# Delta layer of a two-layer decoder trunk: the lower off-diagonal block of the 64-row inverses by a DVE transposition in place of eight matrix products and a copy

## The chip, the cores and the metric

One core of a Trainium2 chip runs the whole program. The metric is device time in microseconds of one execution; three runs of the kernel before gave the median that a changed kernel is held against.

## The reference, cut to what matters

Two layers, a sparse attention and a gated delta rule, each followed by a gated embedding. The change is in the delta rule, where for each head and each chunk of rows a unit lower triangular system is solved:

```python
lower = jnp.where(strict, jnp.einsum("bhntd,bhnjd->bhntj", kb, kc) * decay, 0.0)
a_mat = lower + jnp.eye(CHUNK)
rhs = jnp.concatenate([vc * bc[..., None], kb * jnp.exp(gc)[..., None]], axis=-1)
sol = lax.linalg.triangular_solve(a_mat, rhs, left_side=True, lower=True)
...
def step(state, xs):                      # over the chunks of a head, in order
    u = u_p - w_d @ state
    o = q_d @ state + a_qk @ u
    state = state * cd + k_d.T @ u
```

## The kernel before, in words

The kernel takes chunks of 128 rows, so a half of the sequence has eight chunks per head (NC = 8), and 8 heads times 2 halves make 16 rounds, j = 0 to 15, in the function `phase4`. In a round four things are woven together on the engines' queues: `project(j)` (the products pBk, pBq, pBz, pBv of 128x512, lines L1521 to L1523, three for each of 8 blocks of the input), `within(j-1)` and `beside(j-1)` (the inverses and the other preparations of a head), `across(j-2)` (the recurrence over the chunks: pks, y, pu, uu, po, state, lines L1747 to L1766), and `gated(j-3)` (the output's norm and transposition, pot). Which instruction comes when on an engine follows from the yielded positions and from the scheduler that the program is built with; each engine then takes its own list in order. After the last rounds `ahead` puts the first products of the next stage (poe, L90 to L92) between what is left of the recurrence, and `wout` prepares their weights: an ACT copy (L78, L86) and a subtraction on DVE (L79) or POOL (L87) for each piece of `wo`.

`within` inverts the eight 128x128 triangles of a head at once. The 32x32 diagonal blocks are inverted on DVE (L1632 to L1642), go through DRAM and come back as Uc, the upper triangular form (U), whose transposed blocks are Tc (L1652). Then blocks of 32 are merged to 64, and 64 to 128. With X = (L block) times (T block) on PE (px, L1664, copied by ACT on L1665), the off-diagonal block of U is X-transposed times Uc (pd, L1673, eight products of 32x32 for each p, copied to U by ACT on L1674). For p = 0 the same block is also wanted transposed, in the tile T64, since the merge of 64 to 128 multiplies with it (px_1, L1684, copied by ACT on L1685; pd_2, L1689, copied by ACT on L1690). Before the change that transposed block is computed by itself: eight products more with the operands exchanged (L1677), into the other partitions of the same PSUM tile pd, and a DVE copy (L1678).

Of the kernel before, what the change touches and what calls it, by code (L numbers as in the profile page):

```python
# [27 lines left out]
NC = 8  # L28
# [10 lines left out]
def tile_trunk(ctx: ExitStack, tc: tile.TileContext, a: dict, out: bass.AP):  # L39
    nc = tc.nc  # L40
# [17 lines left out]
    def T(tag, bufs, shape, name, dt=F32, where=None):  # L58
        return (where or pools[-1]).tile(shape, dt, tag=tag, bufs=bufs, name=name)
# [7 lines left out]
    def ps(tag, bufs, name, cols=512):  # L67
        return psum.tile([P, cols], F32, tag=tag, bufs=bufs, name=name)
# [1308 lines left out]
    def phase4():  # L1377
# [10 lines left out]
        T64 = T("T64", 1, [64, NC, 64], "T64")  # L1388
# [164 lines left out]
        def within(j):  # L1553
# [80 lines left out]
            for t in range(0, 32, 2):  # L1634

                n, m_ = t + 2, (t + 1) // 4 + 1
# [9 lines left out]
            Uc, Tc = T("Uc", 1, [P, NC, 32], f"Uc{j}"), T("Tc", 1, [P, NC, 32], f"Tc{j}")  # L1646
# [10 lines left out]
            X = T("tmp", 1, [P, NC, 32], f"X{j}_0")  # L1657
            q = [slice(b * 32, (b + 1) * 32) for b in range(4)]
            for p in range(2):
                e, o = q[2 * p], q[2 * p + 1]  # L1660
# [7 lines left out]
            for p in range(2):  # L1668
                e, o = q[2 * p], q[2 * p + 1]
                yield LV + 0.06 + p * 0.02  # L1670
                pd = ps("g", 3, f"pd{j}_{p}")
                for c in range(NC):
                    nc.tensor.matmul(pd[e, c * 32:(c + 1) * 32], X[o, c], Uc[o, c], start=True, stop=True)  # L1673
                nc.scalar.activation(U[e, :, o], pd[e, :NC * 32].rearrange("p (c n) -> p c n", c=NC), AF.Copy)  # L1674
                if p == 0:
                    for c in range(NC):
                        nc.tensor.matmul(pd[o, 256 + c * 32:256 + (c + 1) * 32], Uc[o, c], X[o, c], start=True, stop=True)  # L1677
                    nc.vector.tensor_copy(T64[o, :, 0:32], pd[o, 256:].rearrange("p (c n) -> p c n", c=NC))  # L1678

            lo, hi = slice(0, 64), slice(64, P)  # L1680
            yield LV + 0.14
            px, X = ps("g", 3, f"px{j}_1"), T("blk", 1, [P, NC, 64], f"X{j}_1")
# [144 lines left out]
        n = 2 * H  # L1827
        for j in range(n + 2):
            o_ = [gated(j - 3, 0.1)] if 3 <= j <= n else []
            if j == n + 1:  # L1830
                o_ = [gated(n - 2, 0.0, True)]
            a_ = [across(j - 2)] if j >= 2 else []
            if j == n + 1:
                a_ = [itertools.chain(a_[0], gated(n - 1, 0.97, True))]
            weave(*a_, *o_, *([within(j - 1), beside(j - 1)] if 1 <= j <= n else []),
                  project(j) if j < n else ahead(j - n))
# [87 lines left out]
```

## Time and profile before

| | |
|---|---|
| three runs, median (lowest to highest) | 3437.28 us (3433.69 to 3441.73) |
| the profiled execution: time, and span in the trace | 3443.02 us, 3441.3 us |
| PE busy, DVE busy, ACT busy, POOL busy | 96%, 61%, 54%, 28% of the span |
| mean granted TensorE clock | 0.982 |
| rounds of the delta stage (from the first L1664 to the last L1689) | 1937 to 3036 us, about 69 us each |

The profiled execution is one run more, with the profiler on. Busy shares are means over a span whose stages differ; the rows that bear on the change are in the section before the prediction.

### The profile page before, as it was taken

To read this page: it belongs to the slowest core of one execution; us is meant where nothing else is said; L and a number is where in the kernel's file an instruction comes from. 1 tells how busy PE (TensorE), PEld (TensorE's weight loads), DVE (VectorE), ACT (ScalarE), POOL (GpSimd) and SP (SyncE) were. 2 spreads that over 40 slices of the span, in tenths; PEclk is the share of its full clock that TensorE was granted. 3 is DMA by queue.
4 is the path that set the end of the run, shared out by engine and by line. 5 is a ranking of instruction groups with operands and counts; after the bars stand their busy time and mean duration, and the time that the engine had idled before them with its cause. 6 is when DMAs were issued, how large, how long until landed. Compare 5 with 4: busy or idle time off the path is not lost.

```text
span 3441.3 us, 51940 instructions
## 1 busy us (share of the span) xinstructions
PE 3304.1 (96%) x18954; PEld 2773.9 (81%) x18954; DVE 2090.1 (61%) x4502; ACT 1862.2 (54%) x3255; POOL 950.1 (28%) x1620
## 2 busy tenths in 40 slices
PE   8999989998899999999999999999999999899999
PEld 6778877887799999888887788887788888678887
DVE  5347996773688888522134577677577677733222
ACT  5356958664677777533335465555565556434221
POOL 2022535246454445211100221231121232321100
PEclk9999999999999999999999999999999999999999
DMA  7532465443422222422222222222222222243212
GB/s 244 178 112 70 128 209 164 168 155 120 152 79 84 79 76 78 159 73 72 66 81 79 51 50 56 53 59 81 62 50 56 53 59 50 86 133 115 74 35 71
DMA packets 327596, 328.46 MB, mean 95 GB/s; under 512 B 69704, under 2 KB 273064, under 8 KB 323240
## 3 DMA queue, kind: packets, MB, share of 16 engines
q1 hardware_dynamic: 327336, 325.11, 31.1%
q8 instruction: 149, 2.44, 0.3%
q14 instruction: 111, 0.91, 0.1%
HBM read 221.24 MB, written 103.81 MB: 94 GB/s over the span
## 4 chain that ended last, share of the span: by engine, by line
PE 54%; DVE 11%; DMA 4%; POOL 2%; ACT 2%; issue 2%; SPq 0%; DVEq 0%; ACTq 0%; POOLq 0%
PE pgm L91 3%; PE pgm L92 3%; PE pgm L90 3%; PE pt L1024 3%; DVE tmp L1639 2%; PE pom L90 2%; PE pom L92 2%; PE pom L91 2%; PE pBv L1521 2%; PE po L1044 2%; PE pBv L1522 2%; PE po L1045 2%; PE lg L92 2%; PE pBv L1523 2%; PE lg L90 2%
## 5 line engine op out<-in xcount | busy, mean ns | idle before, releaser
L79 DVE TENSOR_TENSOR pl<-pt,ph 128x512 fp32r<-128x512 f32 (+1 forms) x288 | 187.7, 658 | 47.3 <-ACT ph L78 45.1
L78 ACT ACTIVATE ph<-pt 128x512 fp32r<-128x512 f32 (+1 forms) x288 | 159.8, 564 | 97.7 <-PE pt L1024 89.0
L1006 ACT ACTIVATE pr<-pr,nm,qscale 128x1024 f32<-128x1024 f32 (+2 forms) x192 | 189.5, 988 | 40.7 <-DVE nm L1003 39.7
L1247 DVE TENSOR_TENSOR gm<-ppm,gm 128x512 f32<-128x512 f32 x64 | 43.4, 690 | 244.3 <-ACT gm L1246 244.3
L423 DVE SCALAR_TENSOR_TENSOR score<-rl,wi,score 128x1024 f32<-128x1024 f32 (+7 forms) x154 | 170.0, 1127 | 35.2 <-ACT rl L415 34.3
L415 ACT ACTIVATE rl<-il 128x1024 f32<-128x1024 f32 (+7 forms) x176 | 142.7, 817 | 74.8 <-PE il L92 69.0
L1024 PE MATMUL pt<-ident,pr 128*128 128x128 f32 x1088 | 169.7, 276 | 8.2 <-ACT pr L1006 5.5
L90 PE MATMUL pom<-wo,ym 128*128 128x512 f32 x432 | 171.1, 396 | 1.9 <-DVE y L1056 1.1
L91 PE MATMUL pom<-wo,ym 128*128 128x512 f32 x432 | 169.4, 392 | 1.3 <-POOL wo L87 1.3
L91 PE MATMUL pgm<-wm,xh 128*128 128x512 f32 x432 | 168.9, 391 | 1.6 <-DVE wm L82 1.6
L729 DVE TENSOR_SCALAR_CACHE_REDUCE tkj<-score,t 128x1664 bf16<-128x1664 f32 (+3 forms) x91 | 121.9, 1353 | 79.0 <-POOL t L769 69.9
L90 PE MATMUL pgm<-wm,xh 128*128 128x512 f32 x432 | 169.0, 391 | 0.7 <-ACT gm L1246 0.6
L92 PE MATMUL pom<-wo,ym 128*128 128x512 f32 x432 | 169.2, 392 | 0.0
L92 PE MATMUL pgm<-wm,xl 128*128 128x512 f32 x432 | 169.0, 391 | 0.0
L1044 PE MATMUL po<-pl,kv 128*128 128x256 f32 x576 | 163.2, 283 | 1.7 <-DVE pl L79 1.6
L1045 PE MATMUL po<-ph,kv 128*128 128x256 f32 x576 | 162.3, 282 | 0.0
L1043 PE MATMUL po<-ph,kv 128*128 128x256 f32 x576 | 161.4, 280 | 0.8 <-ACT ph L78 0.6
L87 POOL TENSOR_TENSOR ym<-yr,ym 128x1024 fp32r<-128x1024 f32 x32 | 77.1, 2409 | 304.7 <-ACT ym L86 304.5
L1246 ACT ACTIVATE gm<-pgm,rm_r 128x512 f32<-128x512 f32 x64 | 42.9, 684 | 183.7 <-PE pgm L91 117.4
L727 ACT ACTIVATE tkj<-score,t 128x1920 bf16<-128x1920 f32 (+3 forms) x91 | 127.8, 1405 | 26.7 <-POOL t L769 13.6
L1752 ACT ACTIVATE qs<-pks,eg 128x128 f32<-128x128 f32 x120 | 44.0, 366 | 179.6 <-DVE y L1749 173.6
L90 PE MATMUL lg<-kv,q 128*128 128x512 f32 (+2 forms) x320 | 139.7, 437 | 0.7 <-DVE mx L997 0.7
(636 smaller groups left out, 10814.6 us busy)
## 6 DMA issues: line engine op xcount, KB each, us to landing
wBr<-in_b_w_in_dram SPq DMA_DIRECT2D x64, 512.0 KB
wr<-in_a_w_in_dram SPq DMA_DIRECT2D x74, 256.0 KB
hT_d<-hT SPq DMA_DIRECT2D x32, 512.0 KB
hz<-hT_d SPq DMA_DIRECT2D x16, 1024.0 KB
yr<-yT_d SPq DMA_DIRECT2D x32, 512.0 KB
x<-in_x_dram SPq DMA_DIRECT2D x16, 512.0 KB
zT_d<-z SPq DMA_DIRECT2D x32, 256.0 KB
k_d<-k SPq DMA_DIRECT2D x16, 512.0 KB
```

What stands on the lines that cost most here:

```text
L78: nc.scalar.activation(hi, src, AF.Copy)
L79: nc.vector.tensor_tensor(lo, src, f32(hi), ALU.subtract)
L90: nc.tensor.matmul(dst, ah, bh, start=first, stop=False)
L91: nc.tensor.matmul(dst, ah, bl, start=False, stop=False)
L92: nc.tensor.matmul(dst, al, bh, start=False, stop=last)
L415: nc.scalar.activation(rl[:, :s1 - s0], pl[:, :s1 - s0], AF.Relu)
L423: nc.vector.scalar_tensor_tensor(sc[:, s0:s1], rl[:, :s1 - s0], w, sc[:, s0:s1], ALU.mult, ALU.add)
L1006: nc.scalar.activation(pr[:, s0:s1], pr[:, s0:s1], AF.Exp, bias=nm, scale=sc, accum_out=den[:, i % 2, x:x + 1])
L1024: nc.tensor.transpose(pt[:, x * P:(x + 1) * P], probs[h, i][:, j * P:(j + 1) * P], ident)
L1043: nc.tensor.matmul(d, V[0][:, j], ph[:, c], start=st, stop=False)
L1044: nc.tensor.matmul(d, V[0][:, j], pl[:, c], start=False, stop=False)
L1045: nc.tensor.matmul(d, V[1][:, j], ph[:, c], start=False, stop=sp)
```

## The change

The eight products L1677 and the copy L1678 go. In their place one DVE transposition of 32x32 blocks reads pd[e], the product that stands in PSUM already for U, and writes T64. Behind it all source lines move up by two, so L1684 of before is L1682 of the changed kernel, L1790 is L1788, and so on.

```diff
                 nc.scalar.activation(U[e, :, o], pd[e, :NC * 32].rearrange("p (c n) -> p c n", c=NC), AF.Copy)
                 if p == 0:
-                    for c in range(NC):
-                        nc.tensor.matmul(pd[o, 256 + c * 32:256 + (c + 1) * 32], Uc[o, c], X[o, c], start=True, stop=True)
-                    nc.vector.tensor_copy(T64[o, :, 0:32], pd[o, 256:].rearrange("p (c n) -> p c n", c=NC))
+                    nc.vector.transpose(T64[o, :, 0:32], pd[e, :NC * 32].rearrange("p (c n) -> p c n", c=NC))
```

On PE, in the round whose products stand at 2019 to 2029 us in the trace (j = 1), the queue holds before (pBv are the products of `project`; of the trace's names the numbers are left out):

```order
L1673 MATMUL pd_0_22236<-Uc_22158,X_0_22189 32x32 x8
L1673 MATMUL pd_1_22261<-Uc_22158,X_0_22189 32x32 x8
L1521 MATMUL pBv_1_22287<-hB_0_20410,wB_22127 128x512
L1522 MATMUL pBv_1_22287<-hB_0_20410,wB_22127 128x512
L1677 MATMUL pd_0_22236<-X_0_22189,Uc_22158 32x32 x8
L1523 MATMUL pBv_1_22287<-hB_0_20410,wB_22127 128x512
L1521 MATMUL pBv_1_22287<-hB_0_20410,wB_22127 128x512
L1522 MATMUL pBv_1_22287<-hB_0_20410,wB_22127 128x512
L1523 MATMUL pBv_1_22287<-hB_0_20410,wB_22127 128x512
L1521 MATMUL pBv_1_22287<-hB_1_20411,wB_22127 128x512
L1684 MATMUL px_1_22298<-T_20782,LT_21695 64x64 x8
```

and with the change:

```order
L1673 MATMUL pd_0_22228<-Uc_22150,X_0_22181 32x32 x8
L1673 MATMUL pd_1_22245<-Uc_22150,X_0_22181 32x32 x8
L1521 MATMUL pBv_1_22271<-hB_0_20410,wB_22119 128x512
L1522 MATMUL pBv_1_22271<-hB_0_20410,wB_22119 128x512
L1523 MATMUL pBv_1_22271<-hB_0_20410,wB_22119 128x512
L1521 MATMUL pBv_1_22271<-hB_0_20410,wB_22119 128x512
L1682 MATMUL px_1_22282<-T_20782,LT_21687 64x64 x8
```

L1677 is gone, and px_1 stands behind four large products after the pd blocks where it stood behind seven; it is the same in most rounds.

On DVE, in the same round, with the engines that each row waits for, before:

```order
L1667 COPY T_20782<-Tc_22159 32x8x32
L1466 SCALAR_TENSOR_TENSOR vT_22176<-xbv_0_22282,b_conv_w,vT_22176 128x512 [waits Activation_49,Pool_49]
L1466 SCALAR_TENSOR_TENSOR vT_22176<-xbv_0_22282,b_conv_w,vT_22176 128x512 [waits DVE_49] x2
L1678 COPY T_20782<-pd_0_22236 32x8x32 [waits PE_49,Activation_49]
L1774 TENSOR_REDUCE ss_22348<-o_22426 128x8 [waits Activation_49]
```

and with the change:

```order
L1667 COPY T_20782<-Tc_22151 32x8x32
L1466 SCALAR_TENSOR_TENSOR vT_22168<-xbv_0_22266,b_conv_w,vT_22168 128x512 [waits Activation_49,Pool_49]
L1466 SCALAR_TENSOR_TENSOR vT_22168<-xbv_0_22266,b_conv_w,vT_22168 128x512 [waits DVE_49]
L1676 STREAM_TRANSPOSE T_20782<-pd_0_22228 32x8x32 [waits Activation_49]
L1466 SCALAR_TENSOR_TENSOR vT_22168<-xbv_0_22266,b_conv_w,vT_22168 128x512 [waits DVE_49]
L1772 TENSOR_REDUCE ss_22332<-o_22410 128x8 [waits Activation_49]
```

The transposition stands one tap of the convolution (L1466) earlier than the copy did, and it waits for ACT, which reads the same block of pd for U.

In the last round (within of j = 15, about 2957 to 2985 us) the lists of POOL, DVE, ACT and PE are put in another order too. On POOL, before (kt and vt are scalings of a head's keys and outputs, wo the weights of the next stage, blk and ym copies for what follows):

```order
L1715 TENSOR_SCALAR kt_31416<-kt_31416,dT_31449 128x128 x8
L87 TENSOR_TENSOR wo_0_31450<-wor_3_31556,wo_0_31450 128x1024
L87 TENSOR_TENSOR wo_4_31577<-wor_5_31628,wo_4_31577 128x1024
L1790 TENSOR_SCALAR vt_30312<-vt_30312,rs_31419 128x128 x8
L87 TENSOR_TENSOR wo_4_31577<-wor_7_31684,wo_4_31577 128x1024
L1712 AFFINE_SELECT aq_31527<-aq_31527 128x1024
```

and with the change:

```order
L1713 TENSOR_SCALAR kt_31296<-kt_31296,dT_31329 128x128 x8
L1788 TENSOR_SCALAR vt_30208<-vt_30208,rs_31299 128x128 x8
L87 TENSOR_TENSOR wo_0_31330<-wor_3_31436,wo_0_31330 128x1024
L87 TENSOR_TENSOR wo_4_31457<-wor_5_31508,wo_4_31457 128x1024
L1710 AFFINE_SELECT aq_31407<-aq_31407 128x1024
L1622 COPY blk_31374<-blk_31374 32x1024 x2
```

The scaling of vt now stands ahead of the pair of wo subtractions instead of behind it. In the same place PE now takes pot and pqs ahead of pu of chunk 1 (it stood behind), and DVE takes a subtraction of its own, wo_4 (L79), ahead of the state of chunk 1 instead of ahead of pot's evictions.

## Rows read from the trace of the kernel before

**Rows 1.** The page: span, and busy time of each engine.

```profile
span 3441.3 us, 51940 instructions
PE 3304.1 (96%) x18954; PEld 2773.9 (81%) x18954; DVE 2090.1 (61%) x4502; ACT 1862.2 (54%) x3255; POOL 950.1 (28%) x1620
```

**Rows 2.** Windows: length, then busy of PE, PEld, DVE, ACT, POOL; clock, DMA.

```profile
1937.00:1956.00 19.00, 18.41 (x113) 13.12 (x114) 4.45 (x7) 3.73 (x7) 2.05 (x7) 0.55 0.15 29
2030.00:2099.00 69.00, 67.73 (x455) 56.29 (x454) 48.51 (x111) 39.09 (x74) 16.89 (x38) 1.00 0.22 55
2970.00:2987.00 17.00, 14.12 (x59) 12.37 (x60) 9.51 (x22) 5.60 (x10) 7.55 (x11) 0.50 0.56 168
3036.00:3441.00 405.00, 397.10 (x1832) 326.37 (x1830) 108.64 (x183) 117.94 (x183) 47.26 (x44) 1.00 0.26 82
```

**Rows 3.** Waits of PE, 1937 to 2957 us: total, times, longest.

```profile
PE pu L1755 <- DVE y L1749: 11.6, 15, 1.0
PE pot L1547 <- POOL vt L1790: 4.8, 12, 0.4
```

**Rows 4.** Timeline of PE in round 1: start, duration, engine, line, operation.

```profile
2021.15 1.09 PE L1673 MATMUL pd<-Uc,X 32*32 32x32 f32 x32
...
2022.51 0.40 PE L1522 MATMUL pBv<-hB,wB 128*128 128x512 f32 x1
2022.84 0.69 PE L1677 MATMUL pd<-X,Uc 32*32 32x32 f32 x16
2023.45 0.50 PE L1523 MATMUL pBv<-hB,wB 128*128 128x512 f32 x1
2023.79 0.39 PE L1521 MATMUL pBv<-hB,wB 128*128 128x512 f32 x1
2024.02 0.40 PE L1522 MATMUL pBv<-hB,wB 128*128 128x512 f32 x1
...
2024.81 1.14 PE L1684 MATMUL px<-T,LT 64*64 64x64 f32 x16
```

**Rows 5.** Timeline of all engines there: DVE and ACT rows.

```profile
2020.23 2.38 DVE L1466 SCALAR_TENSOR_TENSOR vT<-xbv,b_conv_w,vT 128x512 f32<-128x512 f32 x3
...
2021.87 0.78 ACT L1674 ACTIVATE U<-pd 32x256 f32<-32x256 f32 x2 [0.90 <-PE pd L1673]
...
2023.63 0.42 DVE L1678 COPY T<-pd 32x256 f32<-32x256 f32 x1 [1.02 <-PE pd L1677]
```

**Rows 6.** Line L1652, the transposition there is: duration ns min/median/max.

```profile
L1652 DVE STREAM_TRANSPOSE Tc<-Uc x16: 431/432/445, 1937.0 to 3025.6; 128x256 f32<-128x256 f32 x16
```

**Rows 7.** Timeline of PE in round 0, around L1677.

```profile
1946.16 0.63 PE L1523 MATMUL pBv<-hB,wB 128*128 128x512 f32 x1
...
1947.71 0.80 PE L1521 MATMUL pBv<-hB,wB 128*128 128x512 f32 x1
...
1948.31 0.63 PE L1522 MATMUL pBv<-hB,wB 128*128 128x512 f32 x1
1948.73 0.63 PE L1523 MATMUL pBv<-hB,wB 128*128 128x512 f32 x1
```

**Rows 8.** Timeline of PE in round 7, behind L1677.

```profile
2372.88 1.14 PE L1684 MATMUL px<-T,LT 64*64 64x64 f32 x16
2374.80 1.11 PE L1689 MATMUL pd<-U,X 64*64 64x64 f32 x16 [0.77 <-ACT X L1685]
```

**Rows 9.** Timeline of all engines in the last round, 2965 to 2976 us.

```profile
2966.34 4.64 POOL L87 TENSOR_TENSOR wo<-wor,wo 128x1024 fp32r<-128x1024 f32 x2
2966.38 2.34 DVE L1575 TENSOR_TENSOR cj<-cj,bt 128x8 f32<-128x8 f32 x1
...
2968.84 2.17 DVE L1577 TENSOR_SCALAR ncj<-cj 128x8 f32<-128x8 f32 x1
...
2971.40 0.80 PE L1755 MATMUL pu<-y,U 128*128 128x128 f32 x2 [5.38 <-DVE y L1749]
...
2974.91 1.51 PE L1547 MATMUL pot<-ident,vt 128*128 128x128 f32 x4 [1.03 <-POOL vt L1790]
```

**Rows 10.** Lines L1575 and L1577 in all 16 rounds: duration ns min/median/max.

```profile
L1575 DVE TENSOR_TENSOR cj<-cj,bt x16: 161/173/2344, 1873.9 to 2966.4; 128x8 f32<-128x8 f32 x16
...
L1577 DVE TENSOR_SCALAR ncj<-cj x16: 166/239/2173, 1874.2 to 2968.8; 128x8 f32<-128x8 f32 x16
```

## The prediction

> **What bounds the kernel now.** I read the page's first lines first: PE is busy 96% of the span, no other engine over 61% [rows 1]. A busy PE can still be a waiting one, so the windows come next. In a round of the delta stage PE is busy 67.73 of 69 us at full clock, while DVE has some 20 us and ACT 30 us to spare, and the stage behind it is as tight, 397.10 of 405 us [rows 2]. Then the waits: in the fifteen rounds to 2957 us PE waits for DVE's y 11.6 us in all, never over 1.0 at a time, and for POOL's vt 4.8 us [rows 3]. Both waits belong to the start of a round, where each step is released by products of PE itself, so they move with PE. So PE's own list sets the time from here to the end, and a microsecond taken off it in a round should come off the span.
>
> Two places differ. In round 0 PE ran at 0.55 of the clock for 19 us, and in the last round at 0.50 for 17 us [rows 2]. The last round also holds PE's one long idle gap, 5.38 us [rows 9]. The change leaves round 0 as it was but for the products removed; in the last round the lists are put in another order.
>
> **What is removed, on PE.** Sixteen times the eight products L1677. Their price isn't the 0.69 us of the row, which overlaps its neighbours, but the shift of the large products around them. In round 1, L1522 starts at 2022.51 and the second large product behind the block, L1521, at 2023.79: 1.28 us for two steps. Undisturbed, a step is 0.23 us (2023.79 to 2024.02). So the block costs 1.28 - 0.46 = 0.82 us: the products, the change of tile shape on both sides, and a first step behind a small block of 0.34 instead of 0.23 (2023.45 to 2023.79) [rows 4]. Round 1 is the pattern; 14 rounds (1 to 6, 8 to 15) give 14 x 0.82 = 11.5 us.
>
> Round 0 runs at half clock there. From L1523 at 1946.16 to the second large product at 1948.31 are 2.15 us, an undisturbed step is 0.42 (1948.31 to 1948.73), so 2.15 - 0.84 = 1.3 us [rows 7].
>
> In round 7, which has little other work for PE, px_1 is followed by pd_2 1.92 us later, 0.77 of it waiting for ACT's X [rows 8]. ACT's new list has that copy ahead of one convolution scaling that it stood behind, so I add some 0.3 us to the 0.8: 1.1 us.
>
> Sum of the products: 11.5 + 1.3 + 1.1 = 13.9 us.
>
> [...]
>
> **What is added, on DVE.** A transposition of 32x256 out of PSUM, not in the trace. From below: the copy of the same shape out of PSUM takes 0.42 us [rows 5]; the transposition of 128x256 in SBUF 0.43 us [rows 6]. From above I allow their sum, 0.85 us, as if reading PSUM and transposing each took a pass. I take 0.43, since both nearest rows say so. DVE has the room. What counts is when T64 is ready, since px_1 waits for it and PE's whole list stands behind px_1, and the new list has px_1 nearer: four large products behind the pd blocks, not seven.
>
> When PE comes to px_1: L1522 at 2022.51 stays, two more steps of 0.23 give 2022.97, and the change to small tiles 0.33 (2022.51 to 2022.84): 2023.30 [rows 4]. When T64 is ready: the transposition waits for ACT's copy of the same block. ACT starts its two copies at 2021.87 and needs 0.78 for both, so the first ends at 2022.26; DVE has by then finished the two taps that now stand ahead (2020.23 + 2/3 of 2.38 = 2021.82). With 0.1 us from the release to the start (L1677 ended at 2023.53, the copy began at 2023.63) it runs from 2022.36 to 2022.79 [rows 4, 5]. That leaves 0.51 us, and even 0.85 us for the transposition would leave 0.09. So I cost it at nothing; what hides it is pd_1 and the four large products, and without them PE would stand still for about 0.8 us a round.
>
> Behind the transposition on DVE waits the third tap, about 1 us later than now, and then ACT's SiLU of v, now also behind X. Nothing in this round needs v; it is transposed a third of a round later. L1684 to L1689 gets longer by three large products, so X and U are no later than now. The product tile pd is free earlier.
>
> **What is moved: the last round.** Before, two POOL subtractions (L87, 4.64 us for the pair) ran from 2966.34. Two tiny DVE instructions beside them took 2.34 and 2.17 us [rows 9]; in the other rounds they take 0.17 and 0.24 (median of 16) [rows 10]. They ended as one and then the other POOL subtraction ended: DVE was held, 4.1 us in all. Behind them in DVE's list stood y of chunk 1, for which PE idled 5.38 us, and the triangles' rows, then rs, for which POOL's vt and through it PE's pot waited another 1.03 [rows 9]. In the new order vt stands ahead of the POOL pair and needs rs first, so the pair can't run beside these two any more. What is gained isn't 5.38 + 1.03: PE now takes pot ahead of pu, and pot waits for the chain cj, ncj, rs, vt, for which I leave 2 us. 5.38 + 1.03 - 2 = 4.4 us. The 17 us at half clock begin inside that gap [rows 2, 9]; from nothing to 8.5 us (half of 17) could come back. I add 0.6, and take 5 us for the place, bounds -5 to +12.
>
> [...]
>
> **The sum.** 13.9 + 5 = 18.9 us off. The profiled execution took 3443.02 us (span 3441.3 and 1.7 around it), so it would take 3424.1. It is 5.7 us above the median of the runs, 3437.28, and above the slowest of them. Taken off the median: **3418.4, I say 3419 us**. This measurement tells 0.2% (6.9 us) from no change.
>
> **The rivals.**
> 1. *The products go, the last round gives nothing.* The recurrence of the last rounds has few fillers on PE, and y, uu and state can make up a new wait as long as the old one. 3437.3 - 13.9 = 3423. Chance 0.22.
> 2. *The last round gives more:* the stretch at half clock goes with the gap, and later gaps close too. -13.9 - 12: 3411. Chance 0.08.
> 3. *The POOL pair holds DVE again.* Now it runs when DVE comes to its own subtraction of wo_4, two inputs in SBUF, and the state of chunk 1 stands behind that. If both halves of the pair are waited out, 4.64 us [rows 9] are lost where I forecast 5 gained: 3437.3 - 13.9 + 4.6 = 3428. For it: the same kind of row. Against it: the pair is released by vt, and the first half may be over by then. Chance 0.12.
> 4. *T64 comes late.* If the transposition takes longer than 0.43 + 0.51 = 0.94 us, PE stands at px_1 in each round; from 0.94 + 0.82 = 1.76 us the gain is gone. At 1.4 us: 16 x 0.46 = 7.4 lost, 3426 with the last round's 5, 3431 without. Against it: both rows of 0.42 to 0.43. Chance 0.04.
> 5. *The clock falls in each round (slower).* Blocks of small products now follow closer: px, pd and px_1 within 5 us. Round 0 shows low clock through such blocks, 19 us at 0.55 [rows 2]. If 4 us of each of 15 rounds fell to half clock, 2 us each, 30 us are lost: 3437.3 - 18.9 + 30 = 3448. It decides from 1.3 us lost a round (18.9 / 15). Against it: px and pd follow as closely in rounds 1 to 15 today, and the clock is 1.00 there [rows 2]. Chance 0.04.
>
> That the change leaves the products in isn't a rival: they are gone from PE's new list in all sixteen rounds.
>
> **How the numbers follow.** The forecast, with its own range of 3414 to 3423, has 0.50. The range for 8 in 10 takes in rivals 1, 2 and 3 in part: 3409 to 3430. Faster by over 0.2% (under 3430.4): the forecast, rivals 1 and 2, and half of 3, 0.86. Same: the other half of 3 and rival 4, 0.10. Slower: rival 5, 0.04.
>
> **What would show it.** In rounds 1 to 6 the distance from one round's px to the next falls by 0.8 us at the same clock; the transposition lasts 0.4 to 0.45 us and ends ahead of px_1, for which PE shows no wait. In the last round cj and ncj take 0.2 us, and PE's gap ahead of pu of chunk 1 is gone or stands at pot, 2 us long. Wrong would be: a wait of PE for T in each round, a clock under 1.00 in rounds 1 to 6, or a gap of 5 us or more elsewhere in the last round.

## The result, and the profile after

| | before | after |
|---|---|---|
| seven runs each, median (lowest to highest) | 3441.34 us (3433.69 to 3445.08) | 3422.85 us (3419.12 to 3431.99) |
| ratio, 95% interval | | 0.9944, 0.9927 to 0.9961 |
| the profiled execution: time, span | 3443.02 us, 3441.3 us | 3431.10 us, 3429.4 us |

The change made the kernel 18.5 us faster by the medians, and the forecast was 3419 us in a range of 3409 to 3430. The forecast was taken off 3437.28, the median of the first three runs of before; the median of all seven is 4.1 us higher, and the result stands 3.9 above the forecast. The profiled execution is one of the two slowest of its seven, so its span is only 11.9 us shorter; the rows below show where the rest stayed.

The page after, against [rows 1]:

```profile
span 3429.4 us, 51412 instructions
PE 3299.1 (96%) x18698; PEld 2770.9 (81%) x18698; DVE 2088.3 (61%) x4502; ACT 1863.5 (54%) x3255; POOL 953.9 (28%) x1620
```

256 matrix instructions of PE are gone (16 blocks of 16), DVE has as many as it had. Windows after, each from one round's first px to the next one's, so that the length is the round's (rounds 1, 2 and 3, where round j is the one whose px belongs to head and half j; columns as in [rows 2]). What is called the last round, with the gap of 5.38 us, lies by this count behind the px of round 14:

```profile
2010.15:2079.50 69.35, 67.00 (x437) 55.73 (x437) 48.72 (x111) 39.47 (x75) 17.48 (x39) 1.00 0.26 55
2079.50:2152.12 72.62, 71.31 (x436) 59.07 (x436) 48.63 (x111) 38.77 (x74) 17.02 (x39) 0.93 0.22 51
2152.12:2220.31 68.19, 66.93 (x438) 55.71 (x437) 48.52 (x111) 39.12 (x75) 16.98 (x39) 1.00 0.24 55
```

Before, these three took 68.95, 68.97 and 68.98 us. Round 3 is 0.79 shorter, as forecast. Round 1 is longer by 0.40 and round 2 by 3.65: something new stands there. The waits of PE after, 1934 to 2950 us, against [rows 3], name it:

```profile
PE pu L1753 <- DVE y L1747: 11.2, 14, 1.0
PE pot L1547 <- POOL vt L1788: 4.5, 12, 0.4
...
PE px L1664 <- DVE Tc L1652: 1.1, 1, 1.1
```

The waits for y and vt moved with PE, as the forecast said; one wait for Tc, 1.1 us ahead of round 2's px, is new. It isn't a wait of the merge that was changed. More is lost behind the px of round 15: from there to the end are 422.5 us against 415.0 before, with the clock at 0.50 for 20.2 us against 3.8. The stretch from that px to the last product poe, in this profile and then in a second one of the same kernel (e1_after_again, below), which loses nothing there:

```profile
3006.90:3061.16 54.26, 54.15 (x330) 44.62 (x331) 16.94 (x41) 18.69 (x36) 11.04 (x15) 0.91 0.27 90
```

```profile
3006.36:3056.06 49.70, 49.61 (x330) 41.07 (x331) 16.76 (x41) 18.56 (x36) 11.02 (x15) 1.00 0.30 99
```

PE does the same there, and waits for nothing over 0.1 us at that px or behind it; why the clock fell stays open.

The merge itself, in round 3 (timeline, PE, ACT and DVE, against [rows 4, 5]):

```profile
2153.81 1.09 PE L1673 MATMUL pd<-Uc,X 32*32 32x32 f32 x32
...
2154.53 0.78 ACT L1674 ACTIVATE U<-pd 32x256 f32<-32x256 f32 x2 [0.90 <-PE pd L1673]
2154.83 0.50 PE L1521 MATMUL pBv<-hB,wB 128*128 128x512 f32 x1
2154.94 0.44 DVE L1676 STREAM_TRANSPOSE T<-pd 32x256 f32<-32x256 f32 x1 [0.45 <-ACT U L1674]
2155.16 0.40 PE L1522 MATMUL pBv<-hB,wB 128*128 128x512 f32 x1
2155.40 0.39 PE L1523 MATMUL pBv<-hB,wB 128*128 128x512 f32 x1
2155.41 0.75 DVE L1466 SCALAR_TENSOR_TENSOR vT<-xbv,b_conv_w,vT 128x512 f32<-128x512 f32 x1
2155.63 0.40 PE L1521 MATMUL pBv<-hB,wB 128*128 128x512 f32 x1
2155.96 1.14 PE L1682 MATMUL px<-T,LT 64*64 64x64 f32 x16
```

The transposition ends at 2155.38, px_1 starts at 2155.96: 0.58 us to spare, where 0.51 was forecast. Over the 16 rounds (its line in the trace, against [rows 6]) it takes the same time each time:

```profile
L1676 DVE STREAM_TRANSPOSE T<-pd x16: 439/439/440, 1942.0 to 3009.7; 32x256 f32<-32x256 f32 x16
```

The last round after (timeline, 2949 to 2968 us, against [rows 9]):

```profile
2949.68 0.25 DVE L1575 TENSOR_TENSOR cj<-cj,bt 128x8 f32<-128x8 f32 x1
2949.85 1.21 DVE L79 TENSOR_TENSOR wo<-wor,wo 128x1024 fp32r<-128x1024 f32 x1
2950.99 0.15 DVE L1577 TENSOR_SCALAR ncj<-cj 128x8 f32<-128x8 f32 x1
...
2951.77 2.92 PE L1547 MATMUL pot<-ident,vt 128*128 128x128 f32 x8 [1.51 <-POOL vt L1788]
2954.12 4.67 POOL L87 TENSOR_TENSOR wo<-wor,wo 128x1024 fp32r<-128x1024 f32 x2
2958.02 1.85 DVE L79 TENSOR_TENSOR wo<-wor,wo 128x1024 fp32r<-128x1024 f32 x1
...
2964.61 2.11 DVE L79 TENSOR_TENSOR wo<-wor,wo 128x1024 fp32r<-128x1024 f32 x1
...
2967.03 0.49 PE L1745 MATMUL pks<-state,kT 128*128 128x128 f32 x2 [1.63 <-DVE state L1760]
2969.94 0.80 PE L1758 MATMUL po<-uu,kt 128*128 128x128 f32 x2 [1.26 <-ACT uu L1755]
```

cj and ncj take 0.25 and 0.15, the gap of 5.38 ahead of pu is gone, and pot waits 1.51. But DVE's own subtraction of wo takes 1.85 and 2.11 us here instead of 1.21, the state stands behind it and pks waits 1.63; po, behind ACT's uu, waits 1.26.

### The profile page after: what moved, and what is told of

Read it like the earlier page. It is cut to its first block, busy times and chain, and to the rows that moved or that the text cites. A ratio compares the mean times of both kernels' runs of the same rounds, so it can differ in the third digit from the quotient of the medians.

```text
span 3429.4 us, 51412 instructions
## 1 busy us (share of the span) xinstructions
PE 3299.1 (96%) x18698; PEld 2770.9 (81%) x18698; DVE 2088.3 (61%) x4502; ACT 1863.5 (54%) x3255; POOL 953.9 (28%) x1620
## 3 DMA queue, kind: packets, MB, share of 16 engines
q8 instruction: 147, 2.41, 0.3%
## 4 chain that ended last, share of the span: by engine, by line
PE 53%; DVE 11%; DMA 4%; POOL 3%; issue 3%; ACT 2%; SPq 0%; DVEq 0%; ACTq 0%; POOLq 0%
PE pgm L91 3%; PE pgm L90 3%; PE pgm L92 3%; PE pt L1024 3%; DVE tmp L1639 3%; PE pom L90 2%; PE pom L92 2%; PE pom L91 2%; PE po L1044 2%; PE po L1045 2%; PE lg L92 2%; PE lg L90 2%; PE pBv L1521 2%; PE lg L91 2%; PE pBv L1522 2%
## 5 line engine op out<-in xcount | busy, mean ns | idle before, releaser
L79 DVE TENSOR_TENSOR pl<-pt,ph 128x512 fp32r<-128x512 f32 (+1 forms) x288 | 187.7, 658 | 44.8 <-ACT ph L78 42.8
L1639 DVE TENSOR_TENSOR tmp<-inv,blk 128x4 f32<-128x4 f32 (+15 forms) x256 | 138.1, 540 | 5.5
```

What stands on the lines that cost most here:

```text
L79: nc.vector.tensor_tensor(lo, src, f32(hi), ALU.subtract)
L1639: nc.vector.tensor_tensor(w, inv[:, :m_, :n].unsqueeze(2).to_broadcast([P, m_, 2, n]), blk[:, :n, t:n].rearrange("p i t -> p t i").unsquee ...
```

## The experiments

My theory was the sum on record: PE's list is shorter by 0.82 us a round, the transposition is hidden, the last round's new order gives 5. The rivals were that the order gives nothing, that the transposition or the copy counts for itself, and that the new loss in round 2 belongs to the change.

**The change in parts.** The order of the last round hangs on round 14 alone: with the change in rounds 0 to 13 POOL's list there stays that of before, with the change in round 14 alone it is that of after. So two kernels part the products from the order.

```diff
-                if p == 0:
+                if p == 0 and j == 14:      # e8_only14; e9_all_but14: j != 14
                     nc.vector.transpose(T64[o, :, 0:32], ...)
+                elif p == 0:
+                    (the eight products and the copy, as before)
```

> The change in round 14 alone; the others compute the block by products and copy it. The last round's POOL list comes out as with the whole change (vt ahead of the pair of wo subtractions). My theory: 0.82 for the one block and 4 to 5 for the last round, 5 to 6 us off, ratio 0.9983 to 0.9986; cj and ncj take 0.2 us, and the gap of 5.4 us ahead of pu is gone. Rival 1 (the last round's order gives nothing): 0.8 us off, ratio 0.9998. Rival 3 (the pair holds something dearer): 3 to 4 us slower, ratio 1.001.

> The change in all rounds but 14. The last round's POOL list stays that of before (the pair of wo subtractions ahead of vt). My theory: 13.9 - 0.8 = 13.1 us off, ratio 0.9962; cj and ncj take over 2 us again and PE idles some 5.4 us ahead of pu of chunk 1. Rival 1 (the products are all of the gain, the order none): 18 us off, ratio 0.9948.

Measured: round 14 alone 3437.59 us, ratio 0.9999 (0.9983 to 1.0016); all but round 14 3425.94 us, 0.9959 (0.9943 to 0.9974), 14 us off. The second agrees with my sum and leaves rival 1's 0.9948 just inside. The first is nearer to rival 1, so the traces have to tell. In the last round with the change everywhere but in round 14 (timeline):

```profile
2943.78 2.34 DVE L1575 TENSOR_TENSOR cj<-cj,bt 128x8 f32<-128x8 f32 x1
...
2948.80 0.79 PE L1757 MATMUL pu<-y,U 128*128 128x128 f32 x2 [5.38 <-DVE y L1751]
```

and with the change in round 14 alone:

```profile
2955.24 0.24 DVE L1575 TENSOR_TENSOR cj<-cj,bt 128x8 f32<-128x8 f32 x1
...
2972.37 0.49 PE L1749 MATMUL pks<-state,kT 128*128 128x128 f32 x2 [1.63 <-DVE state L1764]
```

The old order brings the old gap back to the hundredth, the new order the new wait. PE's waits in 117 us from the start of that round, as the view of waits adds them up, come to 13.4 us in two kernels with the old order (before and e9_all_but14; before: pu 5.8 and 0.5, pks 5.2, pot 1.0, po 0.9) and to 11.3 and 11.5 with the new one (e19_after_third, a third profile of after, and e8_only14; e19: pks 6.5, po 2.3, pot 1.5, poe 0.6, pu 0.4). From the last pBv, which stands behind round 14's block, to the last poe the old order took 115.2 and 114.5 us (before, e2_products_kept), the new one with the same products 113.5 (e8_only14); without the last block the old one 114.3 (e9_all_but14), the new one 111.8 and 111.9 (e1, e19). So the order gave 1.0 to 2.4 us, about 2, and not 5. All these had 20.5 us at 0.50 in the stretch. Three profiles with the new order had more: 23.9 us (113.4 us, e10_shift64), 30.7 (117.0, the first of after) and 34.1 (119.2, e17_fill, in which a wait for Tc stands there as well). So what the order gave can be lost again to the clock; that the order itself lowers it is not shown, as e1, e8 and e19 have the order and not the loss.

**The copy by itself.** The products stay on PE, read by nobody; the transposition takes the copy's place. PE's order is that of before.

```diff
                     for c in range(NC):
                         nc.tensor.matmul(pd[o, 256 + c * 32:256 + (c + 1) * 32], Uc[o, c], X[o, c], ...)
-                    nc.vector.tensor_copy(T64[o, :, 0:32], pd[o, 256:].rearrange(...))
+                    nc.vector.transpose(T64[o, :, 0:32], pd[e, :NC * 32].rearrange(...))
```

> The eight products are computed as before and read by nobody; only the copy is replaced by the transposition. PE's order is that of before, row for row. My theory, in which only PE's list counts: the time of before, ratio 0.9990 to 1.0010, and no wait of PE for T. Rival (what helps is the copy's earlier end, or DVE's freedom): 2 to 5 us off, ratio 0.9985 to 0.9993, hardly told from none by the time, but px_1 would start earlier behind the last large product. Rival (the transposition costs PE time in each round): 3 to 7 us slower, ratio 1.001 to 1.002, with a wait for T at px_1.

Measured: 3443.14 us, ratio 1.0005 (0.9991 to 1.0019). Neither the copy's removal nor the transposition moves the time; the gain comes with the products that leave PE's list, and with the order that follows from it.

**What a block costs.** One product of eight instead of the change; the other seven blocks of T64's quarter stay zero.

```diff
-                    for c in range(NC):
+                    for c in range(1):
                         nc.tensor.matmul(pd[o, 256 + c * 32:256 + (c + 1) * 32], Uc[o, c], X[o, c], ...)
-                    nc.vector.tensor_copy(T64[o, :, 0:32], pd[o, 256:]...)
+                    nc.vector.tensor_copy(T64[o, 0:1, 0:32], pd[o, 256:288]...)
```

> The kernel before with one product of the eight (and a copy of that one block; the other seven blocks of T64's quarter stay zero). It splits the price of 0.82 us a block into what the products take and what the change of tile shape takes. From the rows of before: 0.10 on the way in (0.33 less a step of 0.23), 0.61 from the block's start to the next large product, 0.11 on the way out. My theory: with one product about 0.21 + 0.61/8 = 0.29 us remain, so px to px in rounds 2 to 5 takes 0.53 us less than before, some 68.45 us. [...]

One run, 3435.43 us; the profile is what counts. Windows, first px to first px, rounds 2 and 3, and the place in round 3 (timeline of PE):

```profile
2078.16:2146.63 68.47, 67.22 (x438) 55.74 (x439) 48.29 (x111) 38.99 (x75) 16.91 (x39) 1.00 0.23 55
2146.63:2215.17 68.54, 67.25 (x439) 55.78 (x439) 48.22 (x111) 39.08 (x75) 16.94 (x39) 1.00 0.25 54
```

```profile
2149.67 0.40 PE L1522 MATMUL pBv<-hB,wB 128*128 128x512 f32 x1
2150.00 0.24 PE L1677 MATMUL pd<-X,Uc 32*32 32x32 f32 x2
...
2150.51 0.40 PE L1521 MATMUL pBv<-hB,wB 128*128 128x512 f32 x1
```

L1522 to the second large product: 0.84 - 2 x 0.23 = 0.38 us remain for a block of one, and the rounds are 0.50 and 0.44 shorter than before, the two behind them 0.42 and 0.45. My theory had 0.29 remaining and was off by 0.09. If each product costs the same, it is (0.82 - 0.38)/7 = 0.063 us and the block of eight 0.50, an estimate; I put the other 0.32 down to the change of tile shape there and back, which no run shows by itself. For comparison, in the trace of before each product is two matrix instructions, and in the rounds from 1 on their starts in L1677 are 0.031 to 0.032 us apart but for the first step, 0.052 to 0.053.

**The wait in round 2.** The changed kernel was profiled twice more.

> The changed kernel once more. My theory (PE's list shorter by 0.82 us in 14 rounds, 2.4 us in rounds 0 and 7, and 4 to 5 us from the new order in the last round, the transposition hidden): 18.9 us off, ratio 0.9945, 0.993 to 0.996. In the first profile of it round 2 lost 4.8 us (PE waited 1.07 us for Tc, then the clock was at 0.50 for 10 us) and the last round lost 5.8 us again behind px_1 at a low clock. If these are chance, the new profile shows px of round 2 to px of round 3 about 0.8 us shorter than before, and no wait for Tc; if the change makes them (the rival), they stand there again at the same places.

> The changed kernel a third time, on the chip of the two before, to hold them against it. My theory, with what the single changes showed (12.3 us for the products that were removed, 2 to 2.5 for the last round's order, 0.9 lost again in round 2): 14 us off, ratio 0.996; the first two measurements gave 0.9944 and 0.9951. Rival (the first sum of 18.9 was right in its terms): 0.9945.

Measured: 3422.80 us, 0.9951 (0.9933 to 0.9969), and 3426.15 us, 0.9952 (0.9937 to 0.9967); the latter lies between its two expectations and decides for neither. Windows of round 1, e1_after_again and then e19_after_third:

```profile
2014.95:2084.04 69.09, 67.00 (x438) 55.71 (x438) 48.56 (x111) 39.43 (x75) 17.48 (x39) 1.00 0.25 55
```

```profile
2015.47:2083.59 68.12, 66.89 (x437) 55.67 (x436) 48.48 (x111) 39.06 (x75) 16.98 (x39) 1.00 0.26 55
```

The first waits 0.86 us for Tc once more, the second not at all; neither has the low clock behind it in round 2, nor the loss behind round 15's px. What differs is among the transfers: between the last step of the inverse and Tc lie four writes to iv_d and the load of Uc (SP's queue), and in the profile of after the load is issued 5.55 us after the first write:

```profile
2070.92 2.52 SPq L1648 DMA_DIRECT2D iv_d<-inv  x4
2076.47 0.37 SPq L1649 DMA_DIRECT2D Uc<-iv_d  x1
```

Before it was 4.02. The transfers in that stretch of after (queue, packets, MB, share of 16 engines):

```profile
q1 hardware_dynamic: 1089, 0.13, 15.7%
q8 instruction: 1, 0.02, 1.3%
```

In the same stretch of before, 2080.99 to 2085.01 us, there is no such line. I take q8 for the queue of PE's instructions, since its packets go with their count: in a whole execution 147 (2.41 MB, 16 KB each) for the 37,396 products and weight loads of after, one for some 254, and 149 for the 512 more of before, one for 256 of these; the other queue of instructions, q14, has 111 in both. If that packet holds up the writes, it is the count of PE's instructions that decides where it falls.

```diff
+                if sb == b == i == 0:                      # before the first product of the program
+                    wt = ps("pp", 4, "wt")
+                    for k in range(16):
+                        nc.tensor.transpose(wt[:, :P], ident, ident)
                 pt = ps("pp", 4, f"xT{sb}_{b}_{i}")
```

> The changed kernel with 16 matrix products more (64 instructions of PE) at the very start, where PE waits 7.5 us for its first data. In three profiles of the changed code PE waits 0.83 to 1.07 us for Tc in round 2, since Uc's load is issued 5.4 to 5.6 us after the inverse instead of 4.04; each time a piece of PE's instructions (16 KB, one for each 256 of its instructions) is fetched 2.1 to 2.3 us ahead of that issue, among the four writes of iv_d. My theory: the fetch holds up the writes, and its place goes by the count of PE's instructions. Then 64 more in front move it 5 to 7 us ahead: in round 2 Uc is issued at 4.04 again, PE's wait for Tc is gone, and px of round 1 to px of round 2 takes 68.1 to 68.2 us instead of 69.0 to 69.1. The wait may turn up in another round where a fetch falls 1 to 4 us ahead of Uc's issue. Rival (a shorter round, not the fetch, makes Uc late): the wait of 0.8 to 1.1 stays in round 2. The time itself: within 2 us of the changed kernel, ratio to before 0.994 to 0.996.

Measured, round 2's stretch, its transfers from the first write to Uc's issue, and the window of round 1:

```profile
2074.23 2.76 SPq L1652 DMA_DIRECT2D iv_d<-inv  x4
2078.48 0.37 SPq L1653 DMA_DIRECT2D Uc<-iv_d  x1
```

```profile
q1 hardware_dynamic: 1094, 0.13, 20.2%
```

```profile
2013.54:2081.66 68.12, 66.88 (x438) 55.71 (x437) 48.43 (x111) 39.09 (x75) 16.70 (x39) 1.00 0.25 55
```

The fetch now starts just ahead of the writes, Uc is issued at 4.25, and the wait is gone: my theory. The fetch moved 3.3 us ahead and not 5 to 7, and the edit adds half of what the expectation says: the trace shows 16 matrix products and 16 weight loads more, 32 instructions and not 64.

The other runs have other counts, and the place of the fetch goes by them. Against before, PE has had 0 instructions fewer when round 2 begins (before, e2, e8), 32 (e10, e17, e18), 56 (e11) or 64 (the other profiles of the changed code), and the fetch starts 5.1 us ahead of the inverse's end, 0.1 ahead to 0.1 behind, 1.6 behind, and 3.2 to 3.6 behind. Only the last count has the wait, in five of six profiles. Over all thirteen profiles of this study, rounds 1 to 14: in 11 Uc was issued more than 4.8 us after the inverse, and in each of these 11 a packet of q8 started 3.1 to 3.6 us after it; in the other 171 none started between 1.7 and 3.5 us after it. The edge is near: in the three profiles of the changed kernel the packet started 3.22, 3.25 and 3.56 us after the inverse, the last without harm, so the same kernel has the wait in one execution and not in the next. It also is no charge on the change alone: with the instruction count of before, or one smaller by nearly a whole packet or a whole one (252 in e11, 256 in e10, e17 and e18), it falls into round 9, and there Uc was late in five of seven profiles (e2, e8, e11, e17, e18; in before and e10 the packet came at 3.57 and 3.64 and did no harm).

The time, 3430.17 us (0.9966, 0.9952 to 0.9981), is no better, and its ratio lies just outside what was expected. The 16 products changed the program's start too: a product some 600 further on in PE's list (nkv) starts at 144.9 us, in the three profiles of the changed kernel at 139.0 to 141.0. The profiled execution is the second fastest of its ten, so it can't show what else the others lost.

**The same 16 products where PE is idle.** They are 32 instructions here too.

```diff
                 px = ps("g", 3, f"px{j}_0{p}")
+                for k in range(16 if j == p == 0 else 0):
+                    nc.tensor.transpose(px[:, :P], ident, ident)
```

> The changed kernel with 16 products of 128x128 more (64 instructions of PE), now in round 0, in front of the first px, where PE waits 2.5 to 2.9 us for Tc in every profile; no other engine's list changes. My theory of the fetches: round 2's wait of 0.8 to 1.1 us for Tc is gone and px to px of round 1 takes 68.1 us, as with the 64 instructions at the start, but without the 6 us that these cost there in the first 150 us. Besides, if the low clock of 3 to 17 us in round 0 follows from that idle stretch, it gets shorter, and round 0, 75 to 80 us in the profiles of the changed code, takes 74 to 76. 1 to 6 us off against the changed kernel, ratio to before 0.9925 to 0.9945. Rival (the products push px back by 1 us or more, or the clock falls all the same): nothing gained, 0.9945 to 0.996.

Measured: 3426.64 us, 0.9951 (0.9935 to 0.9968), no gain. Windows of rounds 0 and 1, and of rounds 3 and 4:

```profile
1928.27:2002.07 73.80, 72.98 (x456) 60.22 (x456) 47.69 (x107) 38.98 (x75) 14.42 (x31) 1.00 0.19 43
2002.07:2070.22 68.15, 66.89 (x437) 55.69 (x436) 48.50 (x111) 39.12 (x75) 16.80 (x39) 1.00 0.26 55
2138.39:2207.78 69.39, 67.01 (x437) 55.72 (x437) 48.58 (x111) 39.47 (x75) 17.55 (x39) 1.00 0.25 55
2207.78:2278.93 71.15, 69.89 (x436) 57.95 (x436) 48.59 (x111) 38.76 (x74) 17.06 (x39) 0.95 0.21 52
```

What was expected came, in rounds 0 (74 us at full clock; whether by the filler stays open, since e10 shows 73.8 without it) and 1. It was given back where fetches fell: in round 4 and the wait ahead of it, 4.3 us against e19, in round 9, 4.5, and behind the px of round 15, 5.9, with 13.7 us at 0.50. The ratio is the rival's.

**The last round's subtractions on DVE.** First those of ym, then those of wo too.

```diff
-        split_sb(yr, y[:, 0], y[:, 1])          # load_y, for the pieces prepared ahead
+        split(yr, y[:, 0], y[:, 1])
-        (split_sb if r % 2 else split)(raw, t[:, 0], t[:, 1])      # wout, e16 only
+        (split_sb if r % 2 and i == 0 else split)(raw, t[:, 0], t[:, 1])
```

> The changed kernel, with the subtraction for the six pieces of ym that are prepared in and behind the last round on DVE (1.2 us each) instead of POOL (2.4 us each). In the last round of the changed kernel three small DVE products of the inverse (L1639) take 2.2 to 2.3 us beside a POOL subtraction of ym, and behind one of them the state of chunk 6 is late: PE waits 2.66 us at pks. My theory: these three take 0.2 to 1.1 us, the wait of 2.66 falls to about 1, the other waits of the last round stay: 1 to 2 us off against the changed kernel, ratio to before 0.9935 to 0.996. Rival (DVE's own subtractions stand ahead of the state instead): the waits add up to as much as they did, 11 us.

> As the one before, and the POOL subtractions of wo (L87, 2.35 us each) on DVE too: POOL holds nothing in the last round. My theory: the wait of 1.63 us at pks and that of 1.2 us at po, which stand behind DVE subtractions that took 1.85 and 2.11 us beside POOL, get shorter; but DVE has four subtractions more of 1.2 us, so the waits add up to 7 to 11 us in place of 11. 0 to 4 us off against the changed kernel, ratio to before 0.993 to 0.996. Rival (DVE's list is now too long in the last round): waits of 12 us or more, 1 to 4 us slower than the changed kernel.

Measured: 3419.23 us, 0.9929 (0.9911 to 0.9947), and 3421.66 us, 0.9944 (0.9922 to 0.9965). With ym on DVE the last L1639 takes 1.11 us instead of 2.22, and the waits for state in the last round (waits of PE) are

```profile
PE pks L1745 <- DVE state L1760: 3.8, 4, 1.6
```

instead of 6.5: the longest, 2.66, fell to 1.32, one of 1.33 ahead of it is gone, and the others stay, as expected. From the last pBv to the last poe it takes 109.7 us, with the same 20.5 us at 0.50 as e1 and e19, which took 111.8 and 111.9: the rows give 2.2 us. The ratio lies just under what was expected, with an interval that reaches into it. With wo on DVE too, PE is idle for 9.7 us from the first px of round 14 to that of round 15, against 8.8 with ym alone and 11.3 to 11.5 without either: in the middle of what was expected, but not as expected. The wait of 1.63 at pks is gone, while those at po grew, from 2.3 us in all to 4.2. Why L1639 takes longer beside POOL is not shown; in the profile of after the one of 2.22 us started at 2993.93, while POOL's subtraction of ym ran from 2992.89 to 2995.27.

Last, e13's change and the 16 products together.

> Both: the 16 products in round 0's idle stretch, and ym's subtractions on DVE, by which the last round's waits fell from 11.3 to 8.8 us. My theory: the two add up, 2.5 us from the last round and 1 to 6 from rounds 0 and 2: 3.5 to 8.5 us off against the changed kernel, ratio to before 0.992 to 0.9938. Rival (what the waits give back is taken by the clock): as the changed kernel, 0.9945.

Measured: 3420.88 us, 0.9943 (0.9925 to 0.9961), with 8.9 us idle in the last round, round 0 at 73.74 and a fetch in round 9. The ratio is nearer to the rival's 0.9945 than to my range. It is 5 us under the changed kernel on the same chip (0.9952), and the intervals overlap: the rows show 2.5 us less waiting (109.4 us from the last pBv to the last poe), the time can't tell it.

## Why the prediction was right, point by point

**What bounds the kernel.** Right: the copy's exchange alone does nothing (1.0005), the products' removal most of it (0.9959 of 0.9944 to 0.9952).

**The products, 13.9 us.** Right in sum, by terms: rounds 1 to 5 gave 0.83 to 0.86 (e19 against before), rounds 7 to 13 0.51 to 1.21, 6.2 in all, round 14 0.83 (from its first px to the last pBv, 10.11 before and 9.28 after), round 15 0.78 (from the last px to the last poe, e9 against before). Round 0, 1.3 forecast, gave 0.75: 79.60 and 79.57 us without the products (e1, e13), 80.33 with them (e8), all three with 13.7 us at 0.50. The place of [rows 8], which the prediction calls round 7, is round 6 when the first is 0; there 1.1 was forecast and 0.76 came (94.82 to 94.06 in e9, both with 10.2 us at 0.50; other profiles with equal time at 0.50 differ there by up to 2 us, so this term is the least sure). 4.2 + 6.2 + 0.83 + 0.78 + 0.75 + 0.76 = 13.5.

**The transposition at nothing.** Right: 0.439 us against 0.43, 0.58 us to spare against 0.51, and its smallest margin in the profile of after is 0.35, at the place of [rows 8]. Rival 4's edge of 0.94, the duration from which px_1 would have waited, was never near.

**The last round, 5 us.** This term was mis-sized: about 2. What the prediction saw came (the gap ahead of pu gone, pot at 1.5 where 2 was left). What it didn't reckon is what the recurrence does next: with pu earlier, the state and uu came to stand behind DVE's own subtractions and ACT's evictions, and pks, po and poe took back 1.3 + 1.4 + 0.6 = 3.3 of 5.4. The 0.6 for the clock came to nothing: 20.5 us at 0.50 in that round in both orders, in the profiles compared above. Rival 3 was there in a small way: beside the POOL pair DVE's subtraction took 1.85 instead of 1.21. This rival names two inputs in SBUF; of the two rows beside the pair of before [rows 9], cj (L1575) has two and took 2.34 us, and ncj (L1577) reads one and took 2.17. Rival 1, nothing from the last round, is nearer to what was found than the forecast's 5.

**The sum.** 13.5 + 2 = 15.5 instead of 18.9. The three measurements of the change gave 18.5, 18.1 and 16.2 us (medians), each with an interval of some 6 to either side, so the time alone would not have found the mis-sized term. That the first of them lies within half a microsecond of 18.9 is luck: the terms don't add up to it. A stretch that the change doesn't touch varies by some 4 us between profiles: the first px of round 0 starts at 1933.6 to 1937.5 us in the three profiles of after, at 1937.6 in that of before and at 1934.5 in e2's.

**The clock, rival 5.** It did not fall for denser small blocks: rounds 1 and 3 to 5 stand at 1.00 after, as before. It fell in round 2, behind the wait for Tc. A clock under 1.00 in rounds 1 to 6 was one of the prediction's signs of being wrong, and it stood in the first profile (0.93); it stood behind the wait that the fetch brings, which the prediction didn't reckon with; e1, with that wait, and e19, without it, have 1.00 there.

## What to carry to other kernels

Price a block of small products by the shift of the large ones around it: here the shift was 0.82 us, of which the products were 0.50 by the estimate from a block of one, and a transposition of 0.44 us on DVE, busy 61% of the span, replaced all of it. When a gap in a chain of dependent steps closes, follow the chain to its next two waits before counting it: here they took back three fifths. Look whether a new wait far from the edit is an old one that moved: here, with 64 PE instructions fewer ahead of round 2, a packet of q8 that had started 5.1 us ahead of the inverse's end started 3.2 to 3.6 behind it, and with the count of before Uc was late in round 9 (e2, e8).

## What the runs showed of the hardware that was not expected

A packet of q8 (16 KB, by the counts above PE's instructions) that started 3.1 to 3.6 us after the inverse, while the writes of iv_d were under way, went with a load of Uc, which waits for them, issued 1.3 to 1.9 us later (11 of 11). Near the upper end it was chance: four that started at 3.56 to 3.72 us did no harm, one at 3.63 did. One at 1.6 cost 0.5.

Behind the 11 late starts, where PE waited about 1 us for Tc ahead of a row of small blocks, the clock was at 0.50 for 6.8 to 13.7 us in 8 cases, and that cost 3 to 6 us more. In the other 145 rounds of that kind (1 to 5 and 7 to 13, thirteen profiles) it fell once, for 3.4 us.
